# A hybrid decoder layer: probabilities of three cross heads turned on VectorE, the last residual added through TensorE, stores in halves

## The chip, the cores and the metric

The kernel runs on one core of one Trainium2 chip. It is one program and one launch. The metric is device time in microseconds (us) of that launch; where several runs were made, the median is given. The core has five engines with their own instruction streams: TensorE (PE, with its weight loads shown apart as PEld), VectorE (DVE), ScalarE (ACT), GpSimd (POOL) and SyncE (SP), which here issues nearly all DMA transfers. Each engine executes in the order in which the program gave it its instructions, and waits on semaphores for the others.

## What is computed

One pre-norm decoder layer for 256 tokens of width 1024, with three gated branches, then a final RMSNorm. All data are float32.

```python
h = rms_norm(x, norm_g)
qa, ka, va, ga, ub, vb, gb, qc, gc, ma, mb, mc = split_cols(h @ w_in)
out_a = moba_attention(rope(qa), rope(ka), va) * silu(ga)      # 6 heads x 128, causal (one block here)
out_b = gmlp_spatial_gate(ub, vb, ...) * silu(gb)              # 6 groups x 128
mem_n = rms_norm(mem, mem_norm_g)
out_c = memory_cross_attention(qc, mem_n, w_mem_kv) * silu(gc) # 4 heads x 128 over 256 memory tokens
y = sigmoid(ma)*(out_a @ w_a) + sigmoid(mb)*(out_b @ w_b) + sigmoid(mc)*(out_c @ w_c)
out = rms_norm(x + y @ w_out, final_norm_g)
```

For a cross head the softmax gives p, tokens by memory tokens (256 by 256); the product p @ v needs p with the memory tokens on the partitions, so p has to be transposed. That is done head by head.

## The kernel before

**Weights.** All weights lie in one DRAM array of 53 pieces of 128 x 2048 float32 (1 MB). The first two are interleaved with the transposed x in the array xw and loaded by `load_st`; the others are loaded by `load(j)` (L169), one transfer each through `load_part` (L165), except piece 2, which comes in two. Three pieces are in SBUF at a time (tag "raw"). A piece is two chunks; each chunk is split into a rounded half hi (ACT, L179) and the remainder lo (DVE, L183), because the products are made of three matmuls in the fp32r format: hi x hi, lo x hi, hi x lo (`mm3`, L332). Four hi and four lo buffers exist, and chunk c+3 is split while chunk c is multiplied.

**Chunks.** `chunks` (L312) lists 106 chunks in the order of TensorE: 82 of the input projection (kinds "tok", output by tokens, and "fea", output by features), 16 of the branch projections ("br", n_br is the index behind them), 8 of the output projection ("out"). The main loop (L912) runs over them: it emits the split of chunk c+3, the load of a piece, then the chunk's matmuls.

**The planner.** All other work (norms, rope, attention heads, gates) is cut into units, each with an engine, a planned duration, what it must follow, and sometimes a chunk by which it is due (`Units`, L68). Before and behind each chunk, `slot` emits the units that fit: an ACT, DVE or POOL unit if its engine, by the planned clock, is no more than 2.5 us ahead of TensorE (0.5 us for POOL), a PE unit if what it follows was done 0.8 us ago by the plan. A unit past its due chunk is emitted as soon as what it follows has been emitted. The plan is made when the program is built; on the chip the order is fixed.

**A cross head** is a chain of units (L736): scores (PE, `c_scores`), row maximum (DVE), exp (ACT), reciprocal of the sum (DVE), normalisation (ACT, L583), transposition of four 128 x 128 blocks on TensorE into a PSUM bank (`c_pT`, L714, through `transpose4`, L551), rounding to pth on ACT (L721), remainder ptl on DVE (`p_lo`, L618, L341), the product with v (PE, `c_pv`, L723), and its copy out (ACT). The next chains wait for parts of this one by `back` (L644).

**Start.** SP and ACT issue the loads of x and of the first weights; meanwhile TensorE runs seven passes of 512 columns and one of 128 on constants (L240), and DVE sets eps (L233); the constant ones is copied on DVE (L309). x by tokens is loaded once as xk (L229) and stays in SBUF to the end, where it is the residual.

**End.** The output projection is made in two halves of the contraction, with the accumulators of both token tiles t and both column halves in PSUM. The last product is t = 1, columns 768 to 1023. `out_part` (L880) adds the residual on DVE (L883) and sums the squares on ACT (L885); `out_gain` multiplies by the gain on POOL for columns 0 to 767; `out_bias` prepares the sum of the earlier parts; `out_store` (L899) takes the square root, the reciprocal, scales the row in three pieces and issues two stores of 128 x 256 and 128 x 768.

Of the kernel before, what the change touches and what calls it, by code (L numbers as in the profile page):

```python
# [124 lines left out]
def tile_hybrid_layer(ctx: ExitStack, tc: tile.TileContext, xw, memT, mem, x, fin_g, ln_g, w, w_sp, b_sp, rope, out):  # L125
# [43 lines left out]
    def load(j):  # L169
        raw_alloc(j)  # L170
        load_part(j, 0, PIECE)

# [54 lines left out]
    load(3)  # L227
    V["xk"] = act.tile([128, 2, D], F32, name="xk", tag="xr")
    nc.sync.dma_start(V["xk"], x)  # L229

    ones = const.tile([128, 128], F32R, name="ones")
    eps = const.tile([128, 1], F32, name="eps")
    nc.vector.memset(eps, EPS)  # L233
    ident = const.tile([128, 128], F32, name="ident")
    make_identity(nc, ident)
    nc.scalar.preload_act_table(AF.Sqrt)

    warm = nc.const_aps.tensor(1.0, (128, 512), BF16)
    wp = bank()
    for n in 7 * [512] + [128]:  # L240
        nc.tensor.matmul(wp[:, 0:n], warm[:, 0:128], warm[:, 0:n], start=True, stop=True)
# [66 lines left out]
    nc.vector.tensor_copy(gains, gain)  # L308
    nc.vector.tensor_copy(ones, nc.const_aps.tensor(1.0, (128, 128), F32))  # L309

# [167 lines left out]
    def setup_consts():  # L478
        nc.sync.dma_start(trig, rope)
        nc.gpsimd.memset(mask, 0.0)  # L480
        nc.gpsimd.affine_select(out=mask[:, 128:256], in_=mask[:, 128:256], pattern=[[-1, 128]], base=0,
                                channel_multiplier=1, compare_op=OP.is_ge, fill=NEG)
# [63 lines left out]
    def rope_b(h):  # L546
        q = V["qk"][0:32, h]
        nc.vector.tensor_tensor(q, q, trig[:, 0, None, :].to_broadcast([32, 2, S]), OP.mult)
        nc.vector.tensor_tensor(q, q, ST["r", h], OP.add)

    def transpose4(p, blocks):  # L551
# [162 lines left out]
    def c_pT(h):  # L714
        p = ST["c", h][0]
        ST["cp", h] = bank()
        transpose4(ST["cp", h], [p[:, hsl(j)] for j in (0, 2, 1, 3)])

    def c_pT_out(h):
        ps = ST["cp", h]  # L720
        nc.scalar.activation(p_tiles("c", h, ps), ps, AF.Copy)  # L721
# [14 lines left out]
    for h in range(HC):  # L736
        U.chain(f"cs{h}", (PE, 0.72, lambda h=h: c_scores(h)), (DVE, 0.9, lambda h=h: c_max(h)),
                (ACT, 1.15, lambda h=h: softmax_exp("c", h)),
                after=[f"qcl{h | 1}", f"mkl{h | 1}", "sqrts"] + back("p", HA + h))
        U.chain(f"cn{h}", (DVE, 0.2, lambda h=h: softmax_sum("c", h)), (ACT, 0.85, lambda h=h: softmax_norm("c", h)),  # L740
                after=[f"cs{h}"])
        U.chain(f"cp{h}", (PE, 0.44, lambda h=h: c_pT(h)), (ACT, 0.62, lambda h=h: c_pT_out(h)),
                after=[f"cn{h}"] + back("v", HA + h))
        U.chain(f"cv{h}", (DVE, 0.68, lambda h=h: p_lo("c", h, 512)), (PE, 0.72, lambda h=h: c_pv(h)),
                (ACT, 0.4, lambda h=h: c_out(h)), after=[f"cp{h}", "mvl0", "mvl1"])
# [28 lines left out]

    def two_split(name, views, after):
        def hi_part():
            src, dh, _ = views()
            nc.scalar.activation(dh, src, AF.Copy)

        def lo_part():  # L780
            src, dh, dl = views()
            nc.vector.tensor_tensor(dl, src, dh.bitcast(F32), OP.subtract)

        U.chain(name, (ACT, 0.6, hi_part), (DVE, 0.68, lo_part), after=after)

    def alloc(*specs):
# [3 lines left out]
        return fn  # L790

    U.add("oaTa", None, 0, lambda: pair("a", "x2", HA), after=["mv.0"])
    for i in range(3):
# [3 lines left out]
        two_split(f"oaT{i}", lambda hs=hs: (V["qk"][:, hs, 0, :], V["ah"][:, hs, :], V["al"][:, hs, :]),  # L797
                  [f"ga_{i}", "oaTa"])
    U.add("ocTa", None, 0, alloc(("och", [128, HC, S], "och", F32R), ("ocl", [128, HC, S], "ocl", F32R)),
# [68 lines left out]
    fb = const.tile([128, 4], F32, name="fb")  # L868

    def mm_out(c, t, a=0, b=512):  # L870
        _, col, k0 = chunks[c]
        n = (col, t, a if (col, t) == (1, 1) else 0)
        if n not in acc:
            acc[n] = bank() if n == (1, 1, 256) or not col else acc_bank()
        for i in range(2):
            k = k0 + i
            mm3(acc[n][:, a:b], V["yh"][:, k, tsl(t)], V["yl"][:, k, tsl(t)],
                hi[c][:, i * 512 + a:i * 512 + b], lo[c][:, i * 512 + a:i * 512 + b], k == 0, k == KD - 1)

    def out_part(col, t, a, b, i):  # L880

        z = V["xk"][:, t, col * 512 + a:col * 512 + b]
        nc.vector.tensor_tensor(z, acc[col, t, a][:, a:b], z, OP.add)  # L883
        jk = work.tile([128, 512], F32, name="jk", tag="p", bufs=3)
# [14 lines left out]
    def out_store(t, n):  # L899
# [4 lines left out]
        z = V["xk"][:, t, :]  # L904
        nc.vector.scalar_tensor_tensor(z[:, 768:D], z[:, 768:D], rf, V["fing"][:, 768:D], op0=OP.mult, op1=OP.mult)  # L905
        nc.scalar.activation(z[:, 0:448], z[:, 0:448], AF.Copy, scale=rf)
        nc.vector.tensor_scalar(z[:, 448:768], z[:, 448:768], rf, None, op0=OP.mult)
        nc.sync.dma_start(out[:, t, 768:D], z[:, 768:D])
        nc.sync.dma_start(out[:, t, 0:768], z[:, 0:768])


    for c in range(n_br + 4):  # L912
        now[0] = c
        s = c + LEAD
        U.slot(c, False)
# [124 lines left out]
```

## Time and profile before

| what | value |
|---|---|
| time, median of 3 runs | 327.27 us (327.12 to 328.14) |
| the profiled execution's own time | 326.89 us |
| its span (first to last instruction) | 325.2 us |
| instructions | 4427 |
| DVE busy | 234.0 us, 72% of the span |
| ACT busy | 201.9 us, 62% |
| POOL busy | 41.9 us, 13% |
| read from HBM, written | 61.55 MB, 1.05 MB |

The profile shows one execution. Its span is 1.7 us shorter than the device time of the same execution; that rest lies outside the program. "Busy" is the time in which at least one instruction of an engine is under way; matmuls are pipelined, so that one of 512 columns shows some 390 ns though the next starts 227 ns later. The chain of waits goes back from the last instruction to what released it, and so tells which engine set the end. Idle time of an engine off that chain costs nothing by itself.

### The profile page before, as it was taken

The numbers are of one execution on the slowest core, as the hardware profiler recorded it, in microseconds if no ns is written. First come the engines' busy times: TensorE is split into PE (matmuls) and PEld (weight loads), VectorE is DVE, ScalarE is ACT, GpSimd is POOL, SyncE is SP. The second block draws the span as 40 slices with busy tenths as digits, with TensorE's granted clock in tenths as the row PEclk, the third lists the DMA queues.
The fourth block names the chain that finished last, engine by engine and source line by source line (L and its number), as shares of the span: only waits on it lengthen the run. The fifth ranks groups of instructions, "written<-read, shape, count | busy, mean of one in ns | idle before, by whom it ended". The sixth has DMA issues, their size and how long they took to land.

```text
span 325.2 us, 4427 instructions
## 1 busy us (share of the span) xinstructions
PE 317.5 (98%) x1660; PEld 271.1 (83%) x1660; DVE 234.0 (72%) x358; ACT 201.9 (62%) x342; POOL 41.9 (13%) x39
## 2 busy tenths in 40 slices
PE   8999999999999999999999999999999999999992
PEld 5888888888889888899888889888888888888881
DVE  4968857896998788989856379794444559768452
ACT  4789786557564756676873986675654633433532
POOL 0008330000000000022000145830000000000022
PEclk9999999999999999999999999999999999999998
DMA  7999796564355463346335176456457463453002
GB/s 261 413 424 413 241 351 222 173 231 142 134 193 190 142 248 130 131 147 240 131 129 197 65 259 192 133 181 216 165 214 243 154 238 141 169 220 129 2 16 113
DMA packets 11012, 62.87 MB, mean 193 GB/s; under 512 B 1232, under 2 KB 2128, under 8 KB 4464
## 3 DMA queue, kind: packets, MB, share of 16 engines
q1 hardware_dynamic: 10560, 62.08, 53.4%
q10 hardware_dynamic: 432, 0.52, 0.5%
q8 instruction: 13, 0.21, 0.2%
q14 instruction: 7, 0.06, 0.0%
HBM read 61.55 MB, written 1.05 MB: 193 GB/s over the span
## 4 chain that ended last, share of the span: by engine, by line
PE 96%; DMA 1%; DVE 1%; ACT 1%; issue 0%; DVEq 0%
PE acc L424 36%; PE acc L333 13%; PE acc L335 13%; PE acc L334 13%; PE aux L333 5%; PE aux L335 5%; PE aux L334 5%; PE acc L364 4%; PE aux L553 2%; DMA st<-in_xw_dram 1%; PE aux L762 1%; PE aux L600 0%; PE aux L639 0%; ACT jk L885 0%; DVE xk L883 0%; DVE xk L905 0%
## 5 line engine op out<-in xcount | busy, mean ns | idle before, releaser
L183 DVE TENSOR_TENSOR lo<-raw,hi 128x1024 fp32r<-128x1024 f32 x102 | 129.3, 1269 | 61.6 <-ACT hi L179 60.9
L179 ACT ACTIVATE hi<-raw 128x1024 fp32r<-128x1024 f32 x102 | 107.8, 1057 | 49.9 <-PE acc L335 39.2
L424 PE MATMUL acc<-n,hi 128*128 128x512 f32 x304 | 79.5, 395 | 0.0
L424 PEld LDWEIGHTS acc<-n,hi 128*128 128x128 f32 x304 | 54.8, 189 | 9.2
L424 PEld LDWEIGHTS acc<-n,lo 128*128 128x128 f32 x304 | 41.5, 190 | 3.0
L424 PE MATMUL acc<-n,lo 128*128 128x256 f32 x304 | 42.4, 282 | 0.0
L333 PE MATMUL acc<-hi,n 128*128 128x512 f32 x80 | 31.2, 390 | 0.0
L334 PE MATMUL acc<-lo,n 128*128 128x512 f32 x80 | 31.1, 389 | 0.0
L335 PE MATMUL acc<-hi,n 128*128 128x512 f32 x80 | 31.1, 389 | 0.0
L699 POOL TENSOR_TENSOR vb<-vb,lng 128x768 f32<-128x768 f32 x2 | 4.5, 2267 | 104.4 <-DVE vb L696 104.4
L335 PEld LDWEIGHTS acc<-hi,n 128*128 128x128 f32 x80 | 15.0, 188 | 3.2
L334 PEld LDWEIGHTS acc<-lo,n 128*128 128x128 f32 x80 | 15.0, 188 | 3.0
L333 PEld LDWEIGHTS acc<-hi,n 128*128 128x128 f32 x80 | 15.0, 188 | 2.9
L889 POOL TENSOR_TENSOR xk<-xk,fing 128x512 f32<-128x512 f32 (+1 forms) x4 | 4.0, 1012 | 100.9 <-ACT jk L885 100.9
L428 ACT ACTIVATE jt<-acc 128x256 f32<-128x256 f32 x14 | 5.4, 384 | 12.4 <-PE acc L424 12.3
L504 POOL TENSOR_TENSOR st<-st,bc 128x256 f32<-128x256 f32 x8 | 9.1, 1168 | 24.0 <-ACT bc L284 24.0
L428 ACT ACTIVATE qk<-acc 128x256 f32<-128x256 f32 x12 | 4.6, 383 | 10.5 <-PE acc L424 10.4
L364 PE MATMUL acc<-hi,h 128*128 128x512 f32 (+1 forms) x34 | 9.3, 400 | 0.3 <-ACT hi L303 0.3
L333 PE MATMUL acc<-hi,a 128*128 128x512 f32 x24 | 9.4, 394 | 0.0
L335 PE MATMUL acc<-hi,a 128*128 128x512 f32 x24 | 9.4, 390 | 0.0
L334 PE MATMUL acc<-lo,a 128*128 128x512 f32 x24 | 9.3, 389 | 0.0
L333 PE MATMUL acc<-hi,obh 128*128 128x512 f32 x24 | 9.3, 389 | 0.0
(217 smaller groups left out, 606.6 us busy)
## 6 DMA issues: line engine op xcount, KB each, us to landing
raw<-in_w_dram SPq DMA_DIRECT2D x50, 1024.0 KB, 4.9
st<-in_xw_dram SPq DMA_DIRECT2D x5, 384.0 KB, 6.1
raw<-in_w_dram SPq DMA_DIRECT2D x2, 512.0 KB, 7.2
xk<-in_x_dram SPq DMA_DIRECT2D x1, 1024.0 KB, 11.2
mt<-in_memT_dram SPq DMA_DIRECT2D x2, 512.0 KB, 8.5
mm<-in_mem_dram SPq DMA_DIRECT2D x2, 512.0 KB, 10.1
out_dram<-xk SPq DMA_DIRECT2D x2, 384.0 KB, 2.5
fing<-in_fin_g_dram SPq DMA_DIRECT2D x1, 512.0 KB, 4.5
```

Of the source, the lines that this page charges most:

```text
L179: nc.scalar.activation(hi[c][:, a:b], raw[c // 2][:, o + a:o + b], AF.Copy)
L183: nc.vector.tensor_tensor(lo[c][:, a:b], raw[c // 2][:, o + a:o + b], hi[c][:, a:b].bitcast(F32), OP.subtract)
L333: nc.tensor.matmul(p, s_hi, m_hi, start=first, stop=False)
L334: nc.tensor.matmul(p, s_hi, m_lo, start=False, stop=False)
L335: nc.tensor.matmul(p, s_lo, m_hi, start=False, stop=last)
L364: nc.tensor.matmul(acc[name, o][t][:, a:b], src[:, k, tsl(t)], wt[c][:, i * 512 + a:i * 512 + b], start=k + n == 0, stop=k == KD - 1 and n ...
L424: nc.tensor.matmul(o, wt, m, start=i == 0, stop=i == len(passes) - 1)
L428: nc.scalar.activation(dst, pa, AF.Copy)
L504: U.add(f"nm{k}", POOL, 1.05, lambda k=k: nc.gpsimd.tensor_tensor(x_k(k), x_k(k), bc["x"], OP.mult), after=["xrms"], due=7)
L553: nc.tensor.transpose(p[:, hsl(j)], src, ident)
L699: nc.gpsimd.tensor_tensor(V["vb"][:, t, :], V["vb"][:, t, :], V["lng"], OP.mult)
L889: nc.gpsimd.tensor_tensor(z, z, V["fing"][:, a:b], OP.mult)
```

## The change

- Heads 0, 1 and 2 of the cross attention: p is transposed on DVE in blocks of 32 x 32 (`c_turn` and `turn_rows`, 16 instructions a head in four units of four), into a tile ct in SBUF that takes the place of xk (tag "xr"). Head 3 stays on TensorE. ACT and DVE read ct where they read the PSUM bank before.
- xk is therefore loaded a second time, at chunk n_br - 8.
- The residual of the last quarter (t = 1, columns 768 to 1023) is split into two halves and added into the accumulator by two matmuls with the identity; the sum of squares and the last scaling read PSUM.
- Each row tile is stored as two halves of 512 columns; the scaling is cut to match.
- Pieces 20 to 29 are loaded in two transfers each. With the second load of xk, 77 transfers become 88.
- Eight warm-up passes of 512 columns in place of seven and one of 128. eps and ones are set on POOL; the mask is cleared in two instructions.
- The split of the gated output of branch a is due two chunks before the last chunk of sig 2.

```diff
     def load(j):
         raw_alloc(j)
-        load_part(j, 0, PIECE)
+        parts = 2 if 20 <= j < 30 else 1
+        for i in range(parts):
+            load_part(j, i * PIECE // parts, (i + 1) * PIECE // parts)
...
-    V["xk"] = act.tile([128, 2, D], F32, name="xk", tag="xr")
-    nc.sync.dma_start(V["xk"], x)
+    def load_x():
+        slot_tile("xk", [128, 2, D], "xr")
+        nc.sync.dma_start(V["xk"], x)
+
+    load_x()
...
-    nc.vector.memset(eps, EPS)
...
+    nc.gpsimd.memset(eps, EPS)
+    nc.gpsimd.tensor_copy(ones, nc.const_aps.tensor(1.0, (128, 128), F32))
...
-    for n in 7 * [512] + [128]:
+    for n in 8 * [512]:
...
-    nc.vector.tensor_copy(ones, nc.const_aps.tensor(1.0, (128, 128), F32))
...
-        nc.gpsimd.memset(mask, 0.0)
+        for t in range(2):
+            nc.gpsimd.memset(mask[:, tsl(t)], 0.0)
...
+    def turn_rows(dst, src, a):
+
+        for b in range(4):
+            nc.vector.transpose(dst(slice(32 * b, 32 * b + 32), slice(32 * a, 32 * a + 32)),
+                                src(slice(32 * a, 32 * a + 32), slice(32 * b, 32 * b + 32)))
...
+    def c_turn(h, a):
+        if h == 0 and a == 0:
+            slot_tile("ct", [128, HC - 1, 512], "xr")
+        p = ST["c", h][0].rearrange("p (t m s) -> p m t s", t=2, m=2)
+        pt = V["ct"][:, h, :].rearrange("p (m t s) -> p m t s", t=2, m=2)
+        turn_rows(lambda r, s: pt[r, :, :, s], lambda r, s: p[r, :, :, s], a)
+        ST["cp", h] = V["ct"][:, h, :]
...
-        U.chain(f"cp{h}", (PE, 0.44, lambda h=h: c_pT(h)), (ACT, 0.62, lambda h=h: c_pT_out(h)),
-                after=[f"cn{h}"] + back("v", HA + h))
+
+        turn = [(DVE, 1.25, lambda h=h, a=a: c_turn(h, a)) for a in range(4)] if h < 3 else             [(PE, 0.44, lambda h=h: c_pT(h))]
+        U.chain(f"cp{h}", *turn, (ACT, 0.62, lambda h=h: c_pT_out(h)), after=[f"cn{h}"] + back("v", HA + h))
...
+    sig2 = chunks.index(("tok", "sig", 1024, 6))
...
-                  [f"ga_{i}", "oaTa"])
+                  [f"ga_{i}", "oaTa"], due=sig2 - 2)
...
+    def residual_parts():
+
+        V["identr"] = work.tile([128, 128], F32R, name="identr", tag="sc", bufs=2)
+        nc.scalar.activation(V["identr"], ident, AF.Copy)
+        V["xks"] = [work.tile([128, 256], F32R, name="xks", tag=g, bufs=2) for g in ("qh", "ql")]
+        split2(V["xk"][:, 1, 768:D], *V["xks"])
+
     def mm_out(c, t, a=0, b=512):
         _, col, k0 = chunks[c]
         n = (col, t, a if (col, t) == (1, 1) else 0)
+        last = n == (1, 1, 256)
         if n not in acc:
-            acc[n] = bank() if n == (1, 1, 256) or not col else acc_bank()
+            acc[n] = bank() if last or not col else acc_bank()
+            if last:
+
+                for i, part in enumerate(V["xks"]):
+                    nc.tensor.matmul(acc[n][:, a:b], V["identr"], part, start=i == 0, stop=False)
...
         z = V["xk"][:, t, col * 512 + a:col * 512 + b]
-        nc.vector.tensor_tensor(z, acc[col, t, a][:, a:b], z, OP.add)
+        if (col, t, a) == (1, 1, 256):
+            z = acc[col, t, a][:, a:b]
+        else:
+            nc.vector.tensor_tensor(z, acc[col, t, a][:, a:b], z, OP.add)
...
         z = V["xk"][:, t, :]
-        nc.vector.scalar_tensor_tensor(z[:, 768:D], z[:, 768:D], rf, V["fing"][:, 768:D], op0=OP.mult, op1=OP.mult)
-        nc.scalar.activation(z[:, 0:448], z[:, 0:448], AF.Copy, scale=rf)
-        nc.vector.tensor_scalar(z[:, 448:768], z[:, 448:768], rf, None, op0=OP.mult)
-        nc.sync.dma_start(out[:, t, 768:D], z[:, 768:D])
-        nc.sync.dma_start(out[:, t, 0:768], z[:, 0:768])
+        last = acc[1, 1, 256][:, 256:512] if t else z[:, 768:D]
+        nc.scalar.activation(z[:, 0:208], z[:, 0:208], AF.Copy, scale=rf)
+        nc.vector.tensor_scalar(z[:, 208:512], z[:, 208:512], rf, None, op0=OP.mult)
+        nc.sync.dma_start(out[:, t, 0:512], z[:, 0:512])
+        nc.scalar.activation(z[:, 512:768], z[:, 512:768], AF.Copy, scale=rf)
+        nc.vector.scalar_tensor_tensor(z[:, 768:D], last, rf, V["fing"][:, 768:D], op0=OP.mult, op1=OP.mult)
+        nc.sync.dma_start(out[:, t, 512:D], z[:, 512:D])
...
+        if c == n_br:
+            residual_parts()
+        if c == n_br - 8:
+
+            load_x()
```

More of the change, by code (lines that the diff above doesn't have):

```diff
@@ L773, in gate_unit, with two_split @@
         nc.gpsimd.tensor_tensor(src, src, g, OP.mult)
-    def two_split(name, views, after):
+    def two_split(name, views, after, due=10 ** 6):
         def hi_part():
@@ L782, in lo_part @@
             nc.vector.tensor_tensor(dl, src, dh.bitcast(F32), OP.subtract)
-        U.chain(name, (ACT, 0.6, hi_part), (DVE, 0.68, lo_part), after=after)
+        U.chain(name, (ACT, 0.6, hi_part), (DVE, 0.68, lo_part), after=after, due=due)
     def alloc(*specs):
@@ L877, in mm_out @@
             mm3(acc[n][:, a:b], V["yh"][:, k, tsl(t)], V["yl"][:, k, tsl(t)],
-                hi[c][:, i * 512 + a:i * 512 + b], lo[c][:, i * 512 + a:i * 512 + b], k == 0, k == KD - 1)
+                hi[c][:, i * 512 + a:i * 512 + b], lo[c][:, i * 512 + a:i * 512 + b], k == 0 and not last, k == KD - 1)
     def out_part(col, t, a, b, i):
         z = V["xk"][:, t, col * 512 + a:col * 512 + b]
-        nc.vector.tensor_tensor(z, acc[col, t, a][:, a:b], z, OP.add)
+        if (col, t, a) == (1, 1, 256):
+            z = acc[col, t, a][:, a:b]
+        else:
+            nc.vector.tensor_tensor(z, acc[col, t, a][:, a:b], z, OP.add)
         jk = work.tile([128, 512], F32, name="jk", tag="p", bufs=3)
```

## The prediction

> **What bounds the kernel now.** I read the page first (busy shares, slices, the chain that ended last), then the waits of TensorE alone, then the chain in order of time around each place that the diff touches.
>
> ```profile
> span 325.2 us, 4427 instructions
> ...
> PE 317.5 (98%) x1660; PEld 271.1 (83%) x1660; DVE 234.0 (72%) x358; ACT 201.9 (62%) x342; POOL 41.9 (13%) x39
> ...
> PE   8999999999999999999999999999999999999992
> ...
> PEclk9999999999999999999999999999999999999998
> ```
>
> ```profile
> PE aux L241 <- PEq L1029: 0.8, 1, 0.8
> PE acc L364 <- ACT hi L303: 0.3, 1, 0.3
> ```
>
> TensorE is busy in every slice, at full granted clock. Over the whole span it waits twice, 1.1 us together and both ahead of its first real matmul. So there is no stall to remove in the middle. The time is a start, then the sum of TensorE's issue times, then a tail behind its last matmul. An edit gains only if it takes passes off TensorE or shortens the tail, and VectorE's share of 72% is room that can be spent.
>
> **Transpositions off TensorE.** In the chain, the groups of line L553 between 154 and 208 us are the four cross heads: eight passes for heads 0 and 1 together, four each for heads 2 and 3.
>
> ```profile
> 166.40 0.87 PE aux L553 x8
> 167.27 0.23 PE acc L333
> ...
> 180.32 0.44 PE aux L553 x4
> ```
>
> Both groups lie on the chain with a matmul directly behind (167.27 is 166.40 + 0.87), so their 0.87 + 0.44 = 1.31 us leave the time in full, if what comes next is ready. Head 3 stays.
>
> What VectorE gets in exchange is 3 x 16 = 48 transpositions of 32 partitions x 128 elements. No row shows one. The nearest is the shuffle, on 32 partitions too:
>
> ```profile
> L541 DVE STREAM_SHUFFLE rs<-qk 32x512 f32<-32x512 f32 x6 | 4.3, 725 | 0.0
> ...
> L770 DVE TENSOR_TENSOR mt<-aux,bsb 128x256 f32<-128x256 f32 x6 | 2.2, 412 | 0.0
> ...
> L271 DVE TENSOR_SCALAR dg<-ident,rstd 128x128 fp32r<-128x128 f32 x2 | 0.6, 284 | 0.1
> ```
>
> ```profile
> 205.68 0.75 DVE L770 TENSOR_TENSOR mt<-aux,bsb 128x256 f32<-128x256 f32 x2
> 154.00:208.00 54.00, 54.00 (x310) 47.27 (x309) 36.45 (x51) 39.40 (x72) 14.69 (x10) 1.00 0.47 164
> ```
>
> From 512 to 256 elements the time falls from 725 to 412 ns across these two kinds, 1.2 ns an element; 128 elements then take some 725 - 384 x 1.2 = 0.26 us, and not less than the 0.28 us of a 128-element TENSOR_SCALAR. I take 0.30. Two neighbours overlap by 0.07 (two of 0.41 in 0.75), so a unit of four takes about 4 x 0.30 - 3 x 0.07 = 1.0 us; the diff plans it at 1.25. Bounds: 0.28 an instruction below, 0.725 above (if a short one costs as much as a long one). 48 of them are 11 to 15 us. In the stretch of the heads VectorE is busy for 36.45 of 54 us (the third pair of columns), so 17.5 us are free and the work fits. At 0.725 it would be 35 us and would run over into the chunks behind.
>
> It must also not make TensorE late. Two things are queued behind the turning on VectorE: the lo halves of the next chunks, and `p_lo`, for which `c_pv` waits in TensorE's fixed order.
>
> ```profile
> L183 DVE TENSOR_TENSOR lo<-raw,hi 128x1024 fp32r<-128x1024 f32 x102 | 129.3, 1269 | 61.6 <-ACT hi L179 60.9
> L179 ACT ACTIVATE hi<-raw 128x1024 fp32r<-128x1024 f32 x102 | 107.8, 1057 | 49.9 <-PE acc L335 39.2
> ...
> 63.36 8.38 PE acc L424 x48
> ```
>
> hi waits for TensorE to free a buffer (39.2 us of its waiting). It is then 1.06 + 1.27 = 2.3 us from the end of chunk c to the finished halves of chunk c+4, which starts three chunks later, 8.38 us: a cushion of 6 us. The planner lets VectorE run at most 2.5 us plus one unit (1.25) ahead before a split is emitted, so 3.8 of the 6 can be used up. No stall from there.
>
> ```profile
> 190.14 0.69 DVE L341 TENSOR_TENSOR ptl<-aux,pth 128x512 fp32r<-128x512 f32 x1
> ...
> 194.59 0.28 PE L333 MATMUL aux<-pth,cx 128*128 128x256 f32 x1
> ```
>
> For head 2 the product starts 3.8 us after its last operand is ready (190.83); the plan itself asks for 0.8. With units at or below the planned 1.25 nothing is late. ACT's rounding reads SBUF in place of PSUM at the same length of 512; L721 stays off the path either way. So this part is -1.31, with 0 as its poor end.
>
> The Trainium skill speaks against this part: "VectorE: DVE Perf Modes", section "Rules for kernel authors", sends a 128 x 128 transposition to TensorE where a PSUM destination will do. Its section "The three transpose paths" gives 390 ns on TensorE and 311 ns on VectorE for bf16. In this trace a block costs TensorE 0.11 us of its stream (0.44 for four), and what the rule means here is rival C below.
>
> **Residual through TensorE.** Two matmuls of 256 columns are added somewhere in the "out" chunks, and the DVE addition behind the last matmul goes.
>
> ```profile
> 316.88 0.12 PE acc L333
> ...
> 318.90 0.34 DVE xk L883
> ...
> 319.27 0.52 ACT jk L885 x2
> ...
> 319.81 0.30 ACT rt L901
> 320.14 0.17 DVE rf L903
> ```
>
> ```profile
> 316.96 0.28 PE L335 MATMUL acc<-hi,y 128*128 128x256 f32 x1
> 317.28 0.42 DVE L883 TENSOR_TENSOR xk<-acc,xk 128x256 f32<-128x256 f32 x1 [0.71 <-PE acc L335]
> 318.40 0.28 PE L335 MATMUL aux<-hi,y 128*128 128x256 f32 x1
> ```
>
> The two passes cost 2 x 0.12 = 0.24 on TensorE. The last matmul ends at 318.68. A reader starts 0.04 later (317.24 to 317.28 one quarter before), so the squares start at 318.72 in place of 319.27: -0.55. Next in line is the bias from DVE (`out_bias`), done at 318.90, when the root wants it at about 319.25; so the full 0.55 counts (bounds -0.4 to -0.6). The split of the residual itself (two ACT copies, one DVE subtraction, about 1.1 us) is emitted at n_br:
>
> ```profile
> 301.59 1.09 ACT L192 ACTIVATE y<-aux 128x512 fp32r<-128x512 f32 x2 [2.10 <-PE aux L553]
> ```
>
> ACT is idle for 2.10 us just there, so it is hidden; without that cover y would be up to 0.7 late, and its first reader is four chunks away.
>
> **Stores.** Scaling and issue take as long as before: ACT two short pieces for one long, DVE a 304 and a 256 piece for a 256 and a 320, SP two issues.
>
> ```profile
> 320.85 0.33 SPq L908 DMA_DIRECT2D out_dram<-xk  x1
> 321.27 0.38 SPq L909 DMA_DIRECT2D out_dram<-xk  x1
> ```
>
> ```profile
> raw<-in_w_dram SPq DMA_DIRECT2D x50, 1024.0 KB, 4.9
> ...
> out_dram<-xk SPq DMA_DIRECT2D x2, 384.0 KB, 2.5
> ...
> out_dram<-xk SPq DMA_DIRECT2D x2, 128.0 KB, 1.9
> ```
>
> By size, 0.6 us for 256 KB, so the last store of 256 KB lands 0.3 earlier if it runs alone; but the one ahead is 128 KB larger by the same amount. I take -0.1, bounds -0.3 and +0.1.
>
> **88 transfers.** Behind the last store, SP passes a fixed row of waits:
>
> ```profile
> L1035 SPq EVENT_SEMAPHORE  x1: 28/28/28, 322.8 to 322.8; - x1
> ...
> L1035 SPq EVENT_SEMAPHORE  x4: 27/28/28, 323.8 to 324.0; - x4
> ```
>
> One ended at 322.8 (the 128 KB store), the next at 323.8 (the last store, 321.27 + 2.5), and three more cost 0.2 us although nothing was outstanding. I infer that eight semaphores are used in turn: 77 = 9 x 8 + 5 leaves three behind the last store, 88 = 11 x 8 leaves none. That is -0.19, bounds -0.19 and +0.06 (if the row's order moves too). The ten extra issues on SP and the second xk (1 MB, queued ahead of one piece, so up to 4.9 later for it) meet buffers asked for about five chunks, 14 us, ahead and landing in 4.9: hidden. Uncovered, it would be a few us once.
>
> **Start.** The seven passes start 0.43 apart and the short one at 3.8; a full eighth ends at 4.2, ahead of the first real matmul.
>
> ```profile
> L241 PE MATMUL aux<-const-bfloat16-1.0 x8: 314/634/634, 0.8 to 3.8; 128*128 128x512 bf16 x7, 128*128 128x128 bf16 x1
> ```
>
> ```profile
> 4.42 1.64 PE L364 MATMUL acc<-hi,h 128*128 128x256 f32 x6 [0.34 <-ACT hi L303]
> ...
> 7.83 0.76 PEld L364 LDWEIGHTS acc<-hi,h 128*128 128x128 f32 x4 [0.37 <-ACT hi L303]
> ```
>
> It fills the 0.34 us gap. What a warmer start would gain before 7.8 us is lost again there, where the weight load waits for hi: 0, bounds -0.2 and 0. The work moved to POOL (13% busy), the halved memset and the due date of branch a's split I cost at 0; POOL and these buffers are idle around them.
>
> **Sum.** -1.31 + 0.24 - 0.55 - 0.10 - 0.19 = -1.91 us. Own time of the profiled execution 326.89 to 325.0 (span 325.2 to 323.3); that execution lies 0.38 below the median of the runs, so the median goes from 327.27 to **325.4**. With the bounds of the terms but the first at its poor end: 324.9 to 326.0.
>
> **The rivals.**
>
> A, the forecast: 325.4. For it: TensorE waits nowhere, so passes that go are time.
>
> B, the heads slide and part of it comes back. Each of three heads lasts some 3 to 4 us longer (4 units for one pass of 0.44), and exp, silu and table load of the last head move with it into other chunks' hi:
>
> ```profile
> 183.06 1.48 DVE L183 TENSOR_TENSOR lo<-raw,hi 128x1024 fp32r<-128x1024 f32 x1 [7.18 <-ACT hi L179]
> ```
>
> Here DVE waited 7.18 us for a hi that stood behind such a lump on ACT, and the cushion of 6 held. A lump one us or so larger would let TensorE wait; that costs about 1.1, the whole net of part one: 326.5.
>
> C, slower: VectorE becomes the bound. If a turning takes 0.725 us, a unit takes 2.7, a head 4 x 1.45 = 5.8 us more than planned; less the 3.8 us found between operand and product, TensorE waits 2.0 us in each of three heads: 325.4 + 6.0 = 331.4. It turns into a loss (over 1.91) from a unit of about 2.35 us, 0.64 an instruction; if only the planned 0.8 stands between, from 1.6, 0.45 an instruction. Against it: the 128-element row above takes 0.284. For it: no row shows the operation.
>
> D, it doesn't do what it says: the stream is paced by the weights' arrival, and freed passes turn into waits. Then 327.2. Against it: SP waits for free buffers, not the reverse.
>
> ```profile
> SPq L167 <- DVE lo L183: 177.4, 35, 8.2
> ```
>
> E, all terms at their good ends, 324.9, and 0.3 more at the start: of the three runs before one took 0.9 us longer than the others (328.14 against 327.12 and 327.27), and if that is the clock opening late behind the 0.34 us gap, a filled gap lowers the median too. 324.6. Against it: at full clock in all slices, the profiled execution, 326.89, is hardly below those two.
>
> **How the numbers follow.** A 0.67, B 0.11, C 0.10, D 0.05, E 0.07. About 0.3% (1.0 us) is what a measurement of this kernel can tell from no change. Faster by more: A and E and a little of B, 0.75; within: B and D, 0.15; slower: C, 0.10. The range runs from E's time to B's upper half, 324.6 to 326.8; it leaves out C, D and a little of E.
>
> **What would show it.** Right: TensorE's waits still two; twelve passes fewer in L553; transpositions near 0.3 us; lo still waiting for hi; ACT's last squares 0.04 behind the last matmul; one wait at SP's end behind the last store. Wrong: a wait of TensorE for DVE ptl or lo between 165 and 210 us, a transposition over 0.45 us, a DVE op still between last matmul and squares.

## The result and the profile after

| | before | after |
|---|---|---|
| time, median of 6 runs each | 327.37 us (327.12 to 328.14) | 325.57 us (324.73 to 325.77) |
| ratio | | 0.9942, 95% interval 0.9928 to 0.9955 |
| profiled execution's own time | 326.89 us | 325.77 us |
| its span | 325.2 us | 324.0 us |

The change takes 1.80 us off. The page of after, with the counts that answer to those of before:

```profile
span 324.0 us, 4493 instructions
...
PE 316.8 (98%) x1650; PEld 270.2 (83%) x1650; DVE 248.0 (77%) x404; ACT 202.6 (63%) x346; POOL 41.6 (13%) x42
...
L185 DVE TENSOR_TENSOR lo<-raw,hi 128x1024 fp32r<-128x1024 f32 x102 | 130.3, 1282 | 47.8 <-ACT hi L181 47.1
...
L560 DVE STREAM_TRANSPOSE ct<-p 32x128 f32<-32x128 f32 x48 | 14.5, 302 | 0.7
```

TensorE has ten passes fewer (twelve transpositions gone, two identity matmuls come, and the warm-up keeps its eight). DVE has 14 us more work, nearly all of it the last row: 48 transpositions at 302 ns. The lo halves still wait for hi, though less (47.1 us where it was 60.9). The waits of TensorE in after (us in total, times, longest):

```profile
PE aux L247 <- PEq L1074: 0.8, 1, 0.8
PE acc L369 <- ACT hi L309: 0.6, 1, 0.6
```

They are still two, both at the start. So neither the turning nor the residual made TensorE wait. To see where the 1.8 us come from, I cut the span at two matmuls which both kernels have: the first of the fifth chunk (line L333 before, L338 after) and the last of all. First before, then after, from the timeline of TensorE (start, length):

```profile
16.13 0.39 PE L333 MATMUL acc<-hi,h 128*128 128x512 f32 x1
```

```profile
16.70 0.39 PE L338 MATMUL acc<-hi,h 128*128 128x512 f32 x1
...
317.95 0.28 PE L340 MATMUL aux<-hi,y 128*128 128x256 f32 x1
```

The start is 0.57 longer (16.13 to 16.70), the stage between is 1.01 shorter (318.40 - 16.13 = 302.27 to 301.26), and behind the last matmul 0.70 goes. The same cuts for every kernel that ran, in us of its profiled execution. "Squares" is from the start of the last matmul to the end of the last reciprocal (rf), "stores" from there to the end of the span:

| kernel | span | start | stage | squares | stores | time, median |
|---|---|---|---|---|---|---|
| before | 325.16 | 16.13 | 302.27 | 1.90 | 4.86 | 327.37 |
| before, once more (c11) | 325.77 | 16.72 | 302.27 | 1.90 | 4.89 | 327.50, one run |
| after | 324.02 | 16.70 | 301.26 | 1.32 | 4.75 | 325.57 |
| c1 after, once more | 323.81 | 16.47 | 301.26 | 1.31 | 4.77 | 325.47 |
| c2 three heads back on TensorE | 324.97 | 16.39 | 302.51 | 1.31 | 4.77 | 327.02 |
| c3 stores as before | 323.34 | 16.48 | 301.26 | 1.32 | 4.29 | 325.11 |
| c4 residual on DVE | 324.59 | 16.89 | 301.03 | 1.91 | 4.76 | 326.10 |
| c5 78 transfers | 324.36 | 16.91 | 301.29 | 1.31 | 4.85 | 326.07, one run |
| c6 POOL as before | 324.03 | 16.17 | 301.42 | 1.32 | 5.12 | 325.74, one run |
| c7 all four heads on DVE | 323.53 | 16.79 | 300.67 | 1.31 | 4.76 | 325.13 |
| c8 every block turned twice | 337.24 | 16.39 | 314.78 | 1.32 | 4.75 | 339.59 |
| c9 same POOL count, other work | 324.52 | 17.18 | 301.26 | 1.31 | 4.76 | 325.61 |
| c10 c7, c3 and c9 together | 322.82 | 16.43 | 300.67 | 1.31 | 4.41 | 324.78 |

One of c10's six executions took 645.96 us at full clock, for a reason that no profile shows; c10's median is 324.78 with it and 324.71 without it.

This table is the instrument of all that follows. Where the code of a stage is the same, its length mostly repeats to 0.03 us: the stage is 301.26 in after, c1, c3 and c9, the squares 1.31 to 1.32. Two values fall out, by 0.16 (the stage of c6) and 0.12 (the stores of c10). The start scatters more, from 16.13 to 17.18 over thirteen profiles, and before itself has 16.13 and 16.72. So a span alone misleads by up to 1 us, while a stage shows 0.2 us in one execution. After's first profile was 0.57 unlucky against before's: without the start the difference is 1.01 + 0.70 = 1.71, near the 1.80 of the medians.

### The profile page after: what moved, and what is told of

Read it like the earlier page. It is cut to its first block, busy times and chain, and to the rows that moved or that the text cites. A ratio compares the mean times of both kernels' runs of the same rounds, so it can differ in the third digit from the quotient of the medians.

```text
span 324.0 us, 4493 instructions
## 1 busy us (share of the span) xinstructions
PE 316.8 (98%) x1650; PEld 270.2 (83%) x1650; DVE 248.0 (77%) x404; ACT 202.6 (63%) x346; POOL 41.6 (13%) x42
## 3 DMA queue, kind: packets, MB, share of 16 engines
HBM read 62.60 MB, written 1.05 MB: 196 GB/s over the span
## 4 chain that ended last, share of the span: by engine, by line
PE 96%; DMA 2%; ACT 1%; ACTq 0%; issue 0%; DVE 0%
PE acc L429 36%; PE acc L340 13%; PE acc L339 13%; PE acc L338 13%; PE aux L338 5%; PE aux L340 5%; PE aux L339 5%; PE acc L369 3%; DMA st<-in_xw_dram 2%; PE aux L565 1%; PE aux L783 1%; PE aux L612 0%; PE aux L651 0%; ACTq L215 0%; ACT hi L309 0%; PE aux L285 0%
## 5 line engine op out<-in xcount | busy, mean ns | idle before, releaser
L185 DVE TENSOR_TENSOR lo<-raw,hi 128x1024 fp32r<-128x1024 f32 x102 | 130.3, 1282 | 47.8 <-ACT hi L181 47.1
L338 PE MATMUL acc<-hi,n 128*128 128x512 f32 x80 | 31.2, 390 | 0.0
L338 PEld LDWEIGHTS acc<-hi,n 128*128 128x128 f32 x80 | 15.0, 188 | 3.0
L560 DVE STREAM_TRANSPOSE ct<-p 32x128 f32<-32x128 f32 x48 | 14.5, 302 | 0.7
L338 PE MATMUL acc<-hi,a 128*128 128x512 f32 x24 | 9.4, 393 | 0.0
```

The source lines that it names most:

```text
L185: nc.vector.tensor_tensor(lo[c][:, a:b], raw[c // 2][:, o + a:o + b], hi[c][:, a:b].bitcast(F32), OP.subtract)
L338: nc.tensor.matmul(p, s_hi, m_hi, start=first, stop=False)
L560: nc.vector.transpose(dst(slice(32 * b, 32 * b + 32), slice(32 * a, 32 * a + 32)), src(slice(32 * a, 32 * a + 32), slice(32 * b, 32 * b + ...
```

## The experiments

The theory was the sum of the prediction. The rivals were that part of the turning is given back (B), and that DVE's margin is thinner than it seems (C). c9, c10 and c11 ran on another chip than c1 to c8.

### c1 and c11: the changed kernel and the kernel before, unedited

> The changed kernel once more, as the control of this group. Theory 1 (the time is start + TensorE's issue times + tail): 325.4 to 325.7 us. If the 0.57 us by which its first profile was later at 16 us is only scatter of the first loads, this profile has TensorE behind the first four chunks anywhere from 16.0 to 16.8 us (before: 16.13, changed: 16.70); if the change causes it, it is at 16.6 to 16.8 again.

> The kernel before once more, for a second profile of its start. Scatter: the end of the first four chunks anywhere from 16.1 to 16.9. POOL's early work as the cause: 16.1 to 16.2 again. Stage 302.27, tail 4.86 in either case.

c1 took 325.47 us, ratio 0.9948 (0.9933 to 0.9962). Its stage, squares and stores agree with after's within 0.03 us; its start is 0.23 shorter. c11 repeats before's stage to the hundredth while its start is 0.59 longer; as it ran on another chip, it does not settle alone that the longer start of after is scatter. The spans of all executions do. Less 309.03 us, which is before's span without its start, the spans of the 17 executions of before that ran beside c1 leave 15.9 to 17.1 us for the start, median 16.7. The six of c1, less 307.34, leave 16.3 to 17.2, median 16.4. These are estimates, as they take the rest to repeat; by them the two starts scatter alike, and the change does not lengthen the start.

### c2: the three heads transposed on TensorE again

```diff
-        turn = [(DVE, 1.25, lambda h=h, a=a: c_turn(h, a)) for a in range(4)] if h < 3 else             [(PE, 0.44, lambda h=h: c_pT(h))]
+        turn = [(DVE, 1.25, lambda h=h, a=a: c_turn(h, a)) for a in range(4)] if h < 0 else             [(PE, 0.44, lambda h=h: c_pT(h))]
```

> Only the turning is undone: all four heads are transposed on TensorE again, everything else of the change stays (second load of xk too). Theory 1: 12 passes come back, 1.2 to 1.3 us slower than c1, TensorE without a wait between 20 and 300 us. Rival (the load on VectorE gives most of it back): less than 0.5 us between the two.

The timeline of TensorE in c2:

```profile
16.39 0.39 PE L338 MATMUL acc<-hi,h 128*128 128x512 f32 x1
...
318.89 0.28 PE L340 MATMUL aux<-hi,y 128*128 128x256 f32 x1
```

The stage is 302.51, which is 1.25 longer than c1's, and nothing else moves by more than 0.1. The time is 327.02 us, ratio to before 0.9994 (0.9981 to 1.0007): without the turning nothing is left that this measurement can tell from no change. Of the 1.80 us the turning is the greater part. c2's stage is 0.24 longer than before's, and c4 below gives 0.23 for the identity matmuls alone. So the second load of xk, the halved transfers and the new due date, which c2 keeps, together neither cost nor bring TensorE's stream anything that shows.

### c3: the stores as before

```diff
-        nc.scalar.activation(z[:, 0:208], z[:, 0:208], AF.Copy, scale=rf)
-        nc.vector.tensor_scalar(z[:, 208:512], z[:, 208:512], rf, None, op0=OP.mult)
-        nc.sync.dma_start(out[:, t, 0:512], z[:, 0:512])
-        nc.scalar.activation(z[:, 512:768], z[:, 512:768], AF.Copy, scale=rf)
         nc.vector.scalar_tensor_tensor(z[:, 768:D], last, rf, V["fing"][:, 768:D], op0=OP.mult, op1=OP.mult)
-        nc.sync.dma_start(out[:, t, 512:D], z[:, 512:D])
+        nc.scalar.activation(z[:, 0:448], z[:, 0:448], AF.Copy, scale=rf)
+        nc.vector.tensor_scalar(z[:, 448:768], z[:, 448:768], rf, None, op0=OP.mult)
+        nc.sync.dma_start(out[:, t, 768:D], z[:, 768:D])
+        nc.sync.dma_start(out[:, t, 0:768], z[:, 0:768])
```

> Only the stores are undone: 128 KB first, then 384 KB, with the old cuts of the scaling. Theory by the traces (the last store of 256 KB landed 2.9 us after its issue, the one of 384 KB 2.5): halves do not pay, the time is within 0.2 us of c1 or up to 0.3 us faster. Rival (the forecast's term): 0.1 to 0.3 us slower than c1.

325.11 us, ratio 0.9932 (0.9918 to 0.9947). From the last reciprocal to the end it takes 4.29 us in place of c1's 4.77: the stores in halves do not save 0.10, they cost 0.48 (0.36 by the medians, with the start in them; up to 0.3 was expected). The DMA issues (KB each, median us from issue to landing), first of after, then of c3:

```profile
out_dram<-xk SPq DMA_DIRECT2D x4, 256.0 KB, 2.8
```

```profile
out_dram<-xk SPq DMA_DIRECT2D x2, 384.0 KB, 2.5
...
out_dram<-xk SPq DMA_DIRECT2D x2, 128.0 KB, 2.0
```

The prediction read the landing time as a line in the size, and so gave 256 KB less than 384 KB. It is more: 2.8 against 2.5. In after the data packets of the last store end about as long behind the reciprocal as in c3 (3.0 to 3.1 us), but the wait on it ends 0.84 us behind its last packet, where in c3 it is 0.47. (The halves are also issued 0.04 us later than the old stores are, counted from the reciprocal.) What differs is the shape: rows of 2 KB in two equal stores, against rows of 3 KB in the later one. Why the completion comes later was not tried.

### c4: the residual added on DVE again

```diff
-        last = n == (1, 1, 256)
+        last = False
...
-        if (col, t, a) == (1, 1, 256):
+        if False:
...
-        last = acc[1, 1, 256][:, 256:512] if t else z[:, 768:D]
+        last = z[:, 768:D]
...
-        if c == n_br:
-            residual_parts()
```

> Only the last residual is undone: VectorE adds it behind the last matmul, the two identity matmuls and the split of the residual go. Theory 1: 0.55 - 0.24 = 0.3 us slower than c1. From the end of the last matmul to the end of the reciprocal 1.6 us in place of 1.04. Rival (the matmuls on the bound engine cost what they bring): within 0.1 us of c1.

326.10 us, ratio 0.9960 (0.9944 to 0.9975). The chain of waits behind the last matmul, first in after, then in c4:

```profile
318.12 0.13 PE aux L340
318.25 0.02 issue
318.27 0.25 ACT jk L923
...
318.78 0.30 ACT rt L939
319.11 0.17 DVE rf L941
```

```profile
318.44 0.34 DVE xk L921
318.80 0.52 ACT jk L923 x2
319.34 0.30 ACT rt L939
319.67 0.17 DVE rf L941
```

In c4 the addition on DVE stands between, as it did before, and "squares" is 1.91, as before; in after the squares begin 0.04 behind the matmul and the DVE step is gone. That is -0.60 of c1 against c4. The stage is 0.23 shorter in c4, the two identity passes. The pair brings 0.37; the medians, with the start in them, differ by 0.63.

### c5: whole transfers for pieces 20 to 29

```diff
-        parts = 2 if 20 <= j < 30 else 1
+        parts = 1
```

> Only the halved loads are undone: 78 transfers in place of 88, one each for pieces 20 to 29. Theory (eight semaphores in turn): the last store's wait is followed by two more at 0.06 us each, so from the end of the last reciprocal to the end of the span 4.76 + 0.12 = 4.88 us. From the end of the first four chunks to the last matmul 301.26 us as in c1. Rival (the waits' order follows the last transfer, or the halves matter for the supply): 4.76 us, or a stage other than 301.26.

326.07 us in a single run. The waits at the end of SP's queue, from the stretch in which the last store is waited for, first in after, then in c5 (xN: number of waits; ns each; first and last start):

```profile
L1080 SPq EVENT_SEMAPHORE  x2: 28/28/28, 322.3 to 323.2; - x2
```

```profile
L1080 SPq EVENT_SEMAPHORE  x3: 28/28/28, 323.4 to 323.5; - x3
```

In after the wait at 323.2 is the last of the row and is the one for the last store. In c5 that one is at 323.4, and two more stand behind it, with nothing outstanding: 78 = 9 x 8 + 6 leaves two of eight. The stores take 4.85 in place of 4.77 and 4.75, which is only 0.08 to 0.10 more, because the wait for the last store itself ends 0.03 earlier behind the reciprocal than in after. By their own starts the waits stand 0.06 us apart, so the two cost 0.13, and the three of before the forecast 0.19. The count of waits behind the store is the one that eight semaphores in turn give. The ten pieces in two transfers show no other effect: the stage is 301.29.

### c6 and c9: what POOL was given

c6 puts eps and ones back on DVE and clears the mask in one instruction, as before. c9 does the first too, but clears the mask in four, so that POOL has as many instructions as in after while its early work is gone. The first diff is common to both; then the mask in c6, and in c9.

```diff
-    nc.gpsimd.memset(eps, EPS)
-    nc.gpsimd.tensor_copy(ones, nc.const_aps.tensor(1.0, (128, 128), F32))
+    nc.vector.memset(eps, EPS)
...
+    nc.vector.tensor_copy(ones, nc.const_aps.tensor(1.0, (128, 128), F32))
```

```diff
-        for t in range(2):
-            nc.gpsimd.memset(mask[:, tsl(t)], 0.0)
+        nc.gpsimd.memset(mask, 0.0)
```

```diff
-        for t in range(2):
-            nc.gpsimd.memset(mask[:, tsl(t)], 0.0)
+        for t in range(4):
+            nc.gpsimd.memset(mask[:, 64 * t:64 * t + 64], 0.0)
```

> eps and ones are set on VectorE again and the mask is cleared by one instruction, so POOL has the instruction count of before; the rest is the changed kernel. The question is the 0.33 us between POOL's last drain and the clearing of the semaphores (0.44 from start to start before, 0.11 changed). Theory (POOL's instruction count decides where its instructions are fetched): the gap is 0.44 again, the tail 5.1 us. Rival (it is scatter or comes from another part): 0.11, the tail 4.76.

> The changed kernel with eps and ones on VectorE as before, but the mask cleared by four instructions, so that POOL still has three instructions more than before, all of them at about 30 us. Two questions. The end: if the count of POOL's instructions sets the gap, it is 0.11 and the tail 4.76; if it was eps or ones, 0.44 and 5.1. The start: the two profiles without eps and ones on POOL (before, c6) have the first four chunks done at 16.13 and 16.17, the seven with them at 16.39 to 16.91. If POOL's early work delays the first loads, it is below 16.3 here and the time 0.2 to 0.5 us under that of c1; if that is scatter of the loads, anywhere from 16.1 to 16.9 and no difference.

c6 took 325.74 us in a single run, but its stores take 5.12, 0.35 more than c1's. (Its stage is 0.16 longer as well. Set beside after matmul by matmul, 0.11 of that falls at one place, 16.7 us; the cause is open.) POOL's clearing of the semaphores at the end of the program and the drain ahead of it, in before, after and c6 (ns each; first and last start):

```profile
L1035 POOLq DRAIN  x1: 78/78/78, 324.3 to 324.3; - x1
...
L1035 POOLq EVENT_SEMAPHORE_RANGE_CLEAR  x1: 96/96/96, 324.8 to 324.8; - x1
```

```profile
L1080 POOLq DRAIN  x1: 78/78/78, 323.5 to 323.5; - x1
...
L1080 POOLq EVENT_SEMAPHORE_RANGE_CLEAR  x1: 96/96/96, 323.6 to 323.6; - x1
```

```profile
L1079 POOLq DRAIN  x1: 78/78/78, 323.2 to 323.2; - x1
...
L1079 POOLq EVENT_SEMAPHORE_RANGE_CLEAR  x1: 96/96/96, 323.6 to 323.6; - x1
```

From one to the other it is 0.44 us in before, 0.11 in after, 0.46 in c6. The clear is followed by some 0.4 us in all three, so the difference counts in full. c9 has 0.11 with the old work on DVE. The page counts 39 instructions on POOL in before, c6 and c11 (which has 0.46), and 42 in the others, which have 0.11: so the gap goes with the number, three more in two different ways, and not with which they are. One or two more were not tried. What the clear waits for is not shown. An 8 KB transfer of instructions begins in before at 325.45 us, 0.29 behind the span's end, and in c6 at 324.31, 0.28 behind it; in after the last one begins at 320.08. So with the three instructions no such transfer stands at the end. But where one does, it begins after the clear, and no run shows that the clear waits for it.

c6 had also a start of 16.17, and one theory was that POOL's early work delays the loads of x. c9 speaks against it: without that work its start is 17.18, the longest of all, and longer than either expectation allowed. So do the estimated starts above, which are no longer in c1, with that work, than in before, without it. The start follows the landing of the third tile of x and weights instead. ACT's roundings that begin with that tile, from ACT's timeline of after, before and c9 (start, length, and in brackets the us waited and for what):

```profile
7.70 1.21 ACT L309 ACTIVATE hi<-st 128x512 fp32r<-128x512 f32 x2 [2.24 <-DMA st<-in_xw_dram]
```

```profile
7.14 1.33 ACT L303 ACTIVATE hi<-st 128x512 fp32r<-128x512 f32 x2 [1.37 <-DMA st<-in_xw_dram]
```

```profile
8.19 1.15 ACT L308 ACTIVATE hi<-st 128x512 fp32r<-128x512 f32 x2 [2.68 <-DMA st<-in_xw_dram]
```

Later by 0.56 and 1.05 than in before, and the starts are later by 0.57 and 1.05: the same shift. In all thirteen profiles the start lies 9.0 to 9.2 us behind that rounding. c9's median, 325.61 us, ratio 0.9941 (0.9920 to 0.9961), is after's.

### c7: the fourth head on DVE too

```diff
-            slot_tile("ct", [128, HC - 1, 512], "xr")
+            slot_tile("ct", [128, HC, 512], "xr")
...
-        turn = [(DVE, 1.25, lambda h=h, a=a: c_turn(h, a)) for a in range(4)] if h < 3 else             [(PE, 0.44, lambda h=h: c_pT(h))]
+        turn = [(DVE, 1.25, lambda h=h, a=a: c_turn(h, a)) for a in range(4)] if h < 4 else             [(PE, 0.44, lambda h=h: c_pT(h))]
```

> Head 3 is turned on VectorE as well. Theory 1: four passes more leave TensorE: from the first four chunks to the last matmul 301.26 - 0.44 = 300.8 us, 325.0 us in all. Rival (VectorE full: the last head comes too late for the spatial gate, which follows it): TensorE waits for VectorE or ACT around 205 to 225 us, and the stage is 301.3 or longer.

325.13 us, ratio 0.9932 (0.9917 to 0.9947). c7's timeline of TensorE, its waits, and its group of transpositions on DVE:

```profile
16.79 0.39 PE L338 MATMUL acc<-hi,h 128*128 128x512 f32 x1
...
317.46 0.28 PE L340 MATMUL aux<-hi,y 128*128 128x256 f32 x1
```

```profile
PE acc L369 <- ACT hi L309: 0.9, 1, 0.9
PE aux L247 <- PEq L1074: 0.8, 1, 0.8
```

```profile
L560 DVE STREAM_TRANSPOSE ct<-p 32x128 f32<-32x128 f32 x64 | 19.4, 302 | 0.9
```

The stage is 300.67: 0.59 less than with three heads, of which the four passes are 0.44; where the other 0.15 comes from is not shown. DVE still has room for it: TensorE waits nowhere in the middle.

### c8: every block turned twice

Each transposition is made twice, so that a unit of turning takes twice as long while the plan and the rest stay.

```diff
-        turn_rows(lambda r, s: pt[r, :, :, s], lambda r, s: p[r, :, :, s], a)
+        for _ in range(2):
+            turn_rows(lambda r, s: pt[r, :, :, s], lambda r, s: p[r, :, :, s], a)
```

> Each of the 48 turnings is done twice, with the same planned 1.25 us a unit; the result is the same. A unit then takes 2.5 us, the size at which rival C of the prediction set the turn into a loss (from 2.36 if 3.8 us lie between operand and product, from 1.6 if only the planned 0.8 us do). By the 3.8: TensorE waits about 4 x 1.25 - 3.8 = 1.2 us in each of three heads, stage 301.26 + 3.6 = 304.9. By the 0.8: 4.2 a head, 313.9. Rival (the cushions hold, since other units between the heads give way): no wait, 301.3.

339.59 us, ratio 1.0371 (1.0345 to 1.0398). A unit takes 2.66 us in c8's timeline of DVE; below it, the waits of TensorE that the other kernels do not have:

```profile
174.35 2.66 DVE L560 STREAM_TRANSPOSE ct<-p 32x128 f32<-32x128 f32 x8
```

```profile
PE aux L339 <- DVE ptl L346: 5.0, 2, 4.4
...
PE aux L338 <- DVE ptl L346: 4.2, 1, 4.2
```

The first two waits are for the remainder ptl of the head, which stands on DVE behind the turning; the third ends with the remainder of head 3, which DVE makes right behind that of head 2. They are 4.4, 0.6 and 4.2 us, 9.2 together. But the stage is 13.5 longer. The first matmul behind the first and the third wait, in c8's timeline of TensorE:

```profile
182.72 0.58 PE L339 MATMUL aux<-ptl,cx 128*128 128x256 f32 x1 [4.35 <-DVE ptl L346]
...
236.04 0.36 PE L338 MATMUL aux<-pth,cx 128*128 128x256 f32 x1 [4.19 <-DVE ptl L346]
```

The windows around the first and the third wait show a part of the rest (busy time of PE, PEld, DVE, ACT, POOL, then the granted clock):

```profile
178.00:183.00 5.00, 0.65 (x5) 0.44 (x4) 4.72 (x12) 1.59 (x3) 0.00 (x0) 0.95 0.00 0
183.00:186.00 3.00, 3.00 (x11) 2.58 (x11) 2.75 (x9) 1.33 (x2) 0.00 (x0) 0.52 0.88 317
...
236.00:240.00 4.00, 3.96 (x17) 3.51 (x18) 3.54 (x8) 1.71 (x3) 3.30 (x2) 0.64 0.26 63
```

While TensorE works again behind the first long wait, it is granted 0.52 of full speed over 3 us, and 0.64 over the 4 us behind the other; in the clock's record it is at half for 3.4 us each time, from 182.5 and from 237.1 us. c8 and after have the same matmuls in the same order, so the loss can be read at each of them. The three waits cost 4.5, 0.8 and 4.35, which is 9.6: a little more than the waits as listed, since these count from the end of a matmul and the next one starts before that. The half clock costs 1.5 and 1.7, and some 0.7 falls in smaller steps, 0.5 of it at two places near 217 and 222 us. That is 13.5. This agrees with the Trainium skill, "TensorE: Matmul & The Clock Gate", section "HAM oscillation — how this bites in real kernels", by which idle gaps of more than some 3.4 us put the clock back to half. Its price does not carry over: in its kernel the clock is throttled for some 1.67 us behind each gap and half of that is lost, where here it was 3.4 us, with 1.5 and 1.7 lost. Behind the wait of 0.6 us some 0.1 is lost. The expectation by the planned 0.8, a stage of 313.9, came within 0.9 of the 314.78, but not for its reason: it had three equal waits of 4.2 and no loss of clock.

### c10: the version that the experiments point to

Four heads on DVE (c7), the stores as before (c3), eps and ones on DVE with the mask in four (c9).

> What paid, together: all four heads turned on VectorE (c7), the old stores (c3), eps and ones on VectorE and the mask in four (c9); the rest of the changed kernel. By the sum of the parts: stage 300.67, tail 4.29, against c1 -0.59 - 0.48 = -1.07: 324.4 to 324.6 us, and up to 0.4 less if c9's start holds. Rival (parts meet, for one VectorE's later ones copy): no faster than c3.

The waits of TensorE in c10:

```profile
PE aux L246 <- PEq L1073: 0.8, 1, 0.8
```

324.78 us, ratio 0.9919 (0.9899 to 0.9939): the lowest median of all, 2.6 below before and 0.8 below after. Stage 300.67 and squares 1.31 are those of c7, the stores with 4.41 lie between c3's 4.29 and c1's 4.77: the issue of the last store took 0.52 us where it took 0.38 in c3, and its packets end 0.12 later. Why is not shown. The median lies 0.2 above the 324.4 to 324.6 expected. Its interval overlaps after's, so the stage table and not the medians carries that it is better: 0.59 in the stage and 0.36 in the stores.

## Why the prediction was right, and where it was not

The time forecast was 325.4; 325.57 was measured. Term by term, in us:

| term | forecast | measured | from |
|---|---|---|---|
| transpositions | -1.31 | -1.25 | stage, c1 against c2 |
| identity matmuls | +0.24 | +0.23 | stage, c1 against c4 |
| squares from PSUM | -0.55 | -0.60 | squares, c1 against c4 |
| stores in halves | -0.10 | +0.48 | stores, c1 against c3 |
| 88 transfers | -0.19 | -0.19 | three waits in before, 0.06 each as in c5 |
| POOL's moves | 0 | -0.35 | stores, c1 against c6 |
| start | 0 | not told from its scatter | spans of before and c1 |
| sum | -1.91 | -1.68; after's own trace against before's, without the start, -1.71 | |

**Right for its own reasons.** The bound was read rightly: TensorE waits nowhere between the first chunk and the last, so passes that leave it are time, and what is behind the last matmul is time. Three terms that carry the sum, 1.62 of the 1.91, hold within 0.06 each. The 0.06 missing at the transpositions were not traced to a cause.

**Right in the sum by cancelling.** The end of the kernel, from the reciprocal on, was forecast at -0.29 and gave -0.11. The traces of before and after show its three parts: the wait for the last store ends 3.93 us behind the reciprocal in place of 3.51 (+0.42; +0.48 between c3 and c1), three waits behind it go (-0.19), and the gap on POOL falls from 0.44 to 0.11 (-0.33). The step that failed is "By size, 0.6 us for 256 KB": it drew a line through two landing times (128 KB and 384 KB) to a store of another row length with another neighbour, and the bound it set, +0.1, came from the same line. The part that offset it, POOL's three additional instructions, was set at 0 because POOL is idle around them. The work is hidden; its count is not, at the end of the program.

**The turning's duration.** 0.30 us an instruction was taken, 302 ns measured. The overlap of 0.07 was wrong: in after twelve take 3.77 us, 0.314 from one to the next. The timeline of DVE, with start and length:

```profile
163.11 3.77 DVE L560 STREAM_TRANSPOSE ct<-p 32x128 f32<-32x128 f32 x12
...
170.60 1.26 DVE L560 STREAM_TRANSPOSE ct<-p 32x128 f32<-32x128 f32 x4
...
214.08 3.77 DVE L560 STREAM_TRANSPOSE ct<-p 32x128 f32<-32x128 f32 x12
...
219.14 1.26 DVE L560 STREAM_TRANSPOSE ct<-p 32x128 f32<-32x128 f32 x4
...
221.57 0.68 DVE L346 TENSOR_TENSOR ptl<-ct,pth 128x512 fp32r<-128x512 f32 x1
222.17 0.69 DVE L346 TENSOR_TENSOR ptl<-aux,pth 128x512 fp32r<-128x512 f32 x1
```

(The line before the last is head 2's remainder, the last one head 3's.) So a unit is 1.26, the planned 1.25, and not 1.0. Nothing hung on it, as any unit up to the planned one leaves the margin whole.

**Rival B: the heads slid, and it cost nothing.** The same lines show how far: head 2, transposed at 180.32 before, is turned between 214 and 220 us, and its product starts at 224.54 in place of 194.59. The windows of the stretch of the heads and of the one behind it, in after, and of the latter in before:

```profile
154.00:208.00 54.00, 54.00 (x286) 46.54 (x285) 43.87 (x77) 38.64 (x67) 13.05 (x8) 1.00 0.48 173
208.00:251.00 43.00, 43.00 (x210) 36.23 (x210) 32.72 (x47) 27.36 (x37) 7.88 (x5) 1.00 0.54 190
```

```profile
208.00:251.00 43.00, 43.00 (x191) 35.62 (x190) 25.35 (x24) 26.01 (x31) 6.36 (x3) 1.00 0.55 189
```

DVE is busy 7.4 us longer in each of them (36.45 to 43.87 and 25.35 to 32.72), and PE is busy for all of both in both kernels. The planner put the additional work where DVE was free. The forecast slide of 3 to 4 us a head was far too small; the forecast that the cushion of lo holds was right. The product of head 2, with its first matmul from the timeline of TensorE, starts 2.3 us after its own ptl is ready (221.57 + 0.68 = 222.25) and 1.7 after head 3's (222.17 + 0.69 = 222.86), which is the last that DVE finishes ahead of it:

```profile
224.54 0.28 PE L338 MATMUL aux<-pth,cx 128*128 128x256 f32 x1
```

For heads 0 and 1 the distance is 2.3 and 3.8 us.

**Rival C: rightly held unlikely, wrongly priced.** The transposition did not take 0.725. But the price assumed for such a case, 331.4 us at a unit of 2.7, took the 3.8 us found between operand and product in one head for the margin of all, and a wait as lost for its length alone. The trace of before has a smaller distance too: for head 3 it is 1.2 us (ptl ready at 198.17, product from 199.35). c8 has a unit of 2.66 and took 339.59. By the prediction's 3.8, a head that is 4 x 1.41 = 5.6 us late would wait 1.8; by the planned 0.8 it would wait 4.8. The three heads waited 4.4, 0.6 and 4.2: two are near the planned margin, and one had more by chance. It is head 1, which has the 3.8 in after. So of the two decision points in the prediction the lower one, 0.45 us an instruction, is the one to work with (no run stands between 0.30 and 0.60), and the clock adds 1.5 to 1.7 us to each wait of over 4.

The rule that spoke against this part, in the Trainium skill, "VectorE: DVE Perf Modes", section "Rules for kernel authors", is not borne out here: c2 is that rule applied, and its stage is 1.25 longer. A block of 128 x 128 costs DVE four instructions, 1.26 us, against 0.11 of TensorE's stream, so the turning is dear; but it is paid by an engine that has time to spare, and the 0.11 by the one that sets the end.

**Rivals D and E.** D (weights pace the stream) falls: c2, c1 and c7 step down with each group of passes. E's better start is not seen: the starts of after's kind lie between 16.17 and 17.18, those of before at 16.13 and 16.72, and the starts estimated from the spans have medians of 16.4 (c1) and 16.7 (before), within their scatter. The eighth warm-up pass alone was not tried.

## What to carry to other kernels

Where one engine waits nowhere, price an edit by the instructions it takes off that engine and off the tail, and check the end of the program apart from the rest: its last store, the waits behind it and the last queue to finish were worth 0.1 to 0.5 us each here, of either sign, and none of them follows from busy shares. A plan fixed at build time gives only the margin that it asks for; a larger distance found in one place is chance, and a wait long enough to drop the clock costs more than its length. To tell effects of 0.2 us where spans scatter by 1 us, cut the trace at instructions that both kernels have and compare the stages.

## What the runs showed of the hardware that was not expected

- Stores of 256 KB in rows of 2 KB land 2.8 us after their issue, and the wait for the last one ends 0.84 us behind its last packet. Stores of 384 KB in rows of 3 KB behind one of 128 KB land in 2.5, with 0.47. The end is 0.48 us later with the smaller rows.
- Three more instructions on POOL, early in the program, go with an end that is 0.33 us shorter: 0.11 in place of 0.44 us between its drain and the clearing of the semaphores (after, c9 against before, c6). The mechanism is open.
- Two waits of over 4 us each brought 3.4 us of half clock (c8), a price of 1.5 and 1.7 us beside the wait; a wait of 0.6 us brought none.
